# Sum of squares, layer-embedding products and row scale at the head of a one-core hybrid decoder layer

## The chip, the cores and the metric

One NeuronCore of a Trainium2 chip. The metric is device time in microseconds of one execution, the median of three runs. The engines are PE (TensorE, matmuls; its weight loads are PEld), VectorE (DVE), ScalarE (ACT), POOL (GpSimd) and SP (SyncE, which here issues the DMAs).

## The reference, cut to what matters

One layer, 512 tokens, width 1024, all in float32:

```python
hn = rms_norm(h, norm_g[i])                    # h * rsqrt(mean(h*h) + eps) * g
z = hn @ w_in[i]                               # q, k, v, gates, pooling and gating inputs
ya = moba_attention(q, k, v, rel_bias) * silu(ga)
yb = multiscale_pool(xb, pool_w[i], pool_scale[i]) * silu(gb)
yc = spatial_gating(uc, vc, sgu_w[i], sgu_b[i]) * silu(gc)
h = h + concat([ya, yb, yc]) @ w_out[i]
h = h + (p[i] @ ple_w[i]) * sigmoid(h @ ple_gate_w[i])
return rms_norm(h, final_g)
```

The change concerns three pieces at the head: the product `p[i] @ ple_w[i]` (512 x 256 by 256 x 1024, the layer embedding), the sum of squares of each row of x, and the row scale `rsqrt(mean + eps)` made from it.

## The kernel before

Every product is made of three float32r matmuls: an operand is cut into a high part (ScalarE copies it to float32r) and a low part (VectorE subtracts the high part), and high*high, high*low and low*high are summed in PSUM (`three`, lines 79 to 81). Activations lie transposed in SBUF, eight blocks `xk[k]` of 128 channels by 512 tokens.

The head runs in this order. Fourteen small matmuls warm PE up. SP loads p and the two halves of the embedding weight (`plw0`, `plw1`: output columns 0 to 511 and 512 to 1023, each with its two blocks of 128 inputs side by side) in pieces, then the eight x blocks, the value weights (`raw_0` to `raw_3`, two x blocks to a weight piece), the bias table and the q and k weights. `raw` tiles take turns in three buffers, so the first value weight waits until p's raw tile has been cut. `cut_into` makes the high and low parts of p and the weights, and `ple_mm` runs the embedding products, four banks `ps_ple0` for the first 512 columns and then `ps_ple1` for the second 512; ScalarE or VectorE copies them to `ple`.

`gain(k)` makes the high and low parts of x times the norm's gain, without the row scale. The value projection (loop over k from 0 to 7, twelve matmuls of 512 columns to a block, banks `ps_v`) runs on these unscaled parts; its rows are scaled when they are copied out (`value`). Meanwhile the row scale is made: ScalarE squares the x blocks (`sq_k`); the squares are added, partly on POOL (`sq_0` to `sq_3`), partly on VectorE; after block `SS_AT` = 3 PE multiplies the sum by a column of ones (`row_scale`, `ps_ss`); VectorE makes the mean plus epsilon (`ms`), POOL its power -0.5 (`rstd`); one block later PE widens `rstd`, one number a row, to a whole tile (`row_scale_wide`, `ps_rbc`), ScalarE copies it to `rbc`, and `rescale(k)` replaces the parts of each block by scaled ones for the q, k and other projections. Each engine runs its instructions strictly in its own order; a framework that schedules ahead of time places them, so that order is not quite the order of the code.

Of the kernel before, what the change touches and what calls it, by code (L numbers as in the profile page):

```python
# [14 lines left out]
AF = mybir.ActivationFunctionType  # L15
ALU = mybir.AluOpType

P = 128
S = 512
D = 1024  # L20
NT = S // P
KD = D // P
# [11 lines left out]
LAG = 4  # L34
HELD = 5
RATE = 1.4
SS_AT = 3


def bucket_ranges():  # L40
# [12 lines left out]
def trunk(ctx: ExitStack, tc: tile.TileContext, t: dict, out: bass.AP):  # L53
    nc = tc.nc
# [7 lines left out]
    pm = pool("pm", bufs=PM, space=bass.MemoryType.PSUM)  # L62
    pa = pool("pa", bufs=8 - PM, space=bass.MemoryType.PSUM)

    def f(ap):
        return ap.bitcast(F32)

    def bank(p, name):
        return p.tile([P, 512], F32, tag="mm" if p is pm else "at", name=name)

    def temp(name, dt=F32):
        return gen.tile([P, 512], dt, tag="t", name=name)

# [28 lines left out]
    def fetch(upto):  # L102
        while len(raws) < min(upto, len(stream)):
            raw = wp.tile([P, 1024], F32, tag="raw", name=f"raw_{len(raws)}")
            nc.sync.dma_start(raw, stream[len(raws)])
            raws.append(raw)

    last_parts, lows = [], []

    def flush():  # L110
        for z in lows:
            z()
        lows.clear()

    def low(hi, lo, raw):
        return lambda: nc.vector.tensor_tensor(lo, raw, f(hi), op=ALU.subtract)  # L116
# [15 lines left out]
    def take(n=1, ahead=3):  # L132
        j = used[0]
        used[0] += n
        flush()
        cut(max(j + n, j + ahead))
        if n > 1:
            flush()
        fetch(len(parts) + 3 - len(lows))
        return parts[j] if n == 1 else parts[j:j + n]  # L140
# [2 lines left out]
    zero = const.tile([P, 256], BF16, name="zero")  # L143
    nc.vector.memset(zero, 0.0)
    pl_raw = [wp.tile([P, 1024], F32, tag="raw", name=f"raw_{n}") for n in ("pT", "plw0", "plw1")]
    first = [slice(0, 256), slice(256, 512), slice(512, 1024)]
    for ks in first:
        nc.sync.dma_start(pl_raw[0][:, ks], t["pT"][:, ks])
        nc.sync.dma_start(pl_raw[1][:, ks], t["plw"][0][:, ks])
    nc.sync.dma_start(pl_raw[2], t["plw"][1])  # L150
    cols = const.tile([P, 10], F32, name="cols")
    nc.sync.dma_start(cols, t["cols"])
    relT = const.tile([HEADS, 32], F32, name="relT")
# [2 lines left out]
    xk = [xt[k // 2][:, (k % 2) * 512:(k % 2 + 1) * 512] for k in range(KD)]  # L156
    for k in range(4):
        nc.sync.dma_start(xk[k], t["xT"][k])
    ident = const.tile([P, P], F32, name="ident")
# [20 lines left out]
    for b, (lo_d, hi_d) in enumerate(bucket_ranges()):  # L180
        n = hi_d - lo_d + 1
        a = 511 - hi_d
# [8 lines left out]
    def gain(k):  # L191
        nc.scalar.activation(hth[:, k, :], xk[k], AF.Copy, scale=cols[:, k:k + 1])
        nc.vector.scalar_tensor_tensor(htl[:, k, :], xk[k], cols[:, k:k + 1], f(hth[:, k, :]), op0=ALU.mult, op1=ALU.subtract)

    pth, ptl = (wp.tile([P, 1024], F32R, tag=n, name=f"{n}_pT") for n in ("hi", "lo"))
    wh0, wl0 = (wp.tile([P, 1024], F32R, tag=n, name=f"{n}_plw0") for n in ("hi", "lo"))
    wh1, wl1 = (wp.tile([P, 1024], F32R, tag=n, name=f"{n}_plw1") for n in ("hi", "lo"))
    ple = [big.tile([P, D], F32, tag="ple", name=f"ple_{i}", bufs=4) for i in range(NT)]

    def ple_mm(ps, i, k, wh, wl, a=0, b=512):  # L200
        c = slice(k * 512 + i * P, k * 512 + (i + 1) * P)
        ks = slice(k * 512 + a, k * 512 + b)
        run(three(ps[:, a:b], pth[:, c], ptl[:, c], wh[:, ks], wl[:, ks], k == 0 and a == 0, k == 1 and b == 512))

    ps0 = [bank(pa, f"ps_ple0{i}") for i in range(NT)]
    for ks in first:
        cut_into(pth[:, ks], ptl[:, ks], pl_raw[0][:, ks])
        cut_into(wh0[:, ks], wl0[:, ks], pl_raw[1][:, ks])
    for i, a in ((0, 0), (1, 0), (2, 0), (3, 0), (0, 256), (1, 256), (2, 256), (3, 256)):
        ple_mm(ps0[i], i, 0, wh0, wl0, a, a + 256)  # L210
    for i, a in ((0, 0), (0, 256), (1, 0), (1, 256), (2, 0), (2, 256), (3, 0), (3, 256)):
        ple_mm(ps0[i], i, 1, wh0, wl0, a, a + 256)
    fetch(1)
    for k in (4, 5):
        nc.sync.dma_start(xk[k], t["xT"][k])
    fetch(2)
    for k in (6, 7):
        nc.sync.dma_start(xk[k], t["xT"][k])
    cut_into(wh1, wl1, pl_raw[2])
    fetch(3)  # L220
    nc.sync.dma_start(tab_d, tab)
    gain(0)
# [10 lines left out]
    for h in range(HEADS):  # L233
        b_t = big.tile([P, 512], F32, tag="B", name=f"bias_{h}", bufs=8)
        nc.sync.dma_start(b_t, bass.AP(tensor=tab_d.tensor, offset=tab_d.offset + h * TW, ap=[[1, P], [1, 512]]))
        bias.append(b_t)
    for i in range(NT):
        ps = bank(pm, f"ps_ple1{i}")
        for k in range(2):
            ple_mm(ps, i, k, wh1, wl1)  # L240
        gain(4 + i)
        nc.vector.tensor_copy(ple[i][:, 512:], ps)

    rstd = const.tile([P, NT], F32, name="rstd")
    rbc = temp("rbc")
    sq_t = [temp(f"sq_{k}") for k in range(KD)]

    def square(k):  # L250
        nc.scalar.activation(sq_t[k], xk[k], AF.Square)

    def add_up(eng, a, b):
        eng.tensor_tensor(a, a, b, op=ALU.add)

    def row_scale():
        ps = bank(pm, "ps_ss")
        for i in range(NT):
            nc.tensor.matmul(ps[:, i:i + 1], sq_t[7][:, i * P:(i + 1) * P], ones, start=True, stop=True)
        ms = const.tile([P, NT], F32, name="ms")  # L260
        nc.vector.tensor_scalar(ms, ps[:, :NT], 1.0 / D, EPS, op0=ALU.mult, op1=ALU.add)
        nc.gpsimd.tensor_tensor(rstd, ms, half, op=ALU.pow)

    def row_scale_wide():
        ps = bank(pm, "ps_rbc")
        for i in range(NT):
            nc.tensor.matmul(ps[:, i * P:(i + 1) * P], rstd[:, i:i + 1].to_broadcast([P, P]), ident, start=True, stop=True)
        nc.scalar.activation(rbc, ps, AF.Copy)

    def rescale(k):  # L270
        hn = temp(f"hn_{k}")
        nc.vector.scalar_tensor_tensor(hn, xk[k], cols[:, k:k + 1], rbc, op0=ALU.mult, op1=ALU.mult)
        nc.scalar.activation(hth[:, k, :], hn, AF.Copy)
        return low(hth[:, k, :], htl[:, k, :], hn)
# [13 lines left out]
    for k in range(KD):  # L288
        if k % 2 == 0:
            wh, wl = take(ahead=2)  # L290
            flush()
        if k == 0:
            for z in range(4):
                square(z)
            add_up(nc.gpsimd, sq_t[0], sq_t[1])
            add_up(nc.gpsimd, sq_t[0], sq_t[2])
        elif k == 1:
            square(4)
            square(5)
            add_up(nc.gpsimd, sq_t[0], sq_t[3])  # L300
            add_up(nc.vector, sq_t[5], sq_t[4])
        elif k == 2:
            square(6)
            square(7)
            add_up(nc.vector, sq_t[6], sq_t[5])
            add_up(nc.vector, sq_t[7], sq_t[6])
            add_up(nc.vector, sq_t[7], sq_t[0])
        elif k >= 5:
            for z in ((0, 1, 2), (3,), (4, 5))[k - 5]:
                lows.append(rescale(z))  # L310
                if len(lows) > 1:
                    lows.pop(0)()
        kk = k % 2
        for i in range(NT):
            run(three(vps[i], hth[:, k, i * P:(i + 1) * P], htl[:, k, i * P:(i + 1) * P],
                      wh[:, kk * 512:(kk + 1) * 512], wl[:, kk * 512:(kk + 1) * 512], k == 0, k == KD - 1))
        if k == SS_AT:
            row_scale()
        if k == SS_AT + 1:
            row_scale_wide()  # L320
    for k in (6, 7):
        lows.append(rescale(k))
        lows.pop(0)()
    flush()


# [394 lines left out]
    ps = [bank(pm, f"ps_h{m}") for m in range(2)]  # L721
# [9 lines left out]
    for m in range(2, KD):  # L731
        w = take()
        ps = bank(pm, f"ps_h{m}")
# [32 lines left out]
    ps = [bank(pa, f"ps_g0{i}") for i in range(NT)]  # L766
    for c in range(4):
        wh, wl = take()
        for k in (2 * c, 2 * c + 1):
            z = slice((k % 2) * 512, (k % 2 + 1) * 512)  # L770
# [42 lines left out]
    for i in range(NT - 1):  # L813
        ps = ticking(second(i, 0, 512, 0))
        side.append(finish(i, ps))
    i = NT - 1
    nc.gpsimd.tensor_tensor(h2[i, 0], h2[i, 0], fg[:, :512], op=ALU.mult)
    a, b = h2[i, 1][:, :256], h2[i, 1][:, 256:]
    ps = ticking(second(i, 0, 256, 0))
# [92 lines left out]
```

## Time and profile before

| What | us |
|---|---|
| median of three runs | 301.58 (301.19 to 302.85) |
| profiled execution, its own time | 301.06 |
| span of the profiled execution | 299.3 |
| PE busy | 287.9 (96%) |
| VectorE busy | 206.5 (69%) |
| ScalarE busy | 176.6 (59%) |
| POOL busy | 37.2 (12%) |

The span runs from the first to the last instruction; the profiled execution's time is 1.8 us more. A busy PE is not a PE at its peak: matmuls overlap, so what one costs is read from start to start. The granted clock of TensorE stands in the profile as a share of full speed: 1.00 is 2.4 GHz, 0.50 is 1.2 GHz. Its mean over the span is 0.987.

### The profile page before, as it was taken

To read this page: it belongs to the slowest core of one execution; us is meant where nothing else is said; L and a number is where in the kernel's file an instruction comes from. 1 tells how busy PE (TensorE), PEld (TensorE's weight loads), DVE (VectorE), ACT (ScalarE), POOL (GpSimd) and SP (SyncE) were. 2 spreads that over 40 slices of the span, in tenths; PEclk is the share of its full clock that TensorE was granted. 3 is DMA by queue.
4 is the path that set the end of the run, shared out by engine and by line. 5 is a ranking of instruction groups with operands and counts; after the bars stand their busy time and mean duration, and the time that the engine had idled before them with its cause. 6 is when DMAs were issued, how large, how long until landed. Compare 5 with 4: busy or idle time off the path is not lost.

```text
span 299.3 us, 4228 instructions
## 1 busy us (share of the span) xinstructions
PE 287.9 (96%) x1452; PEld 242.0 (81%) x1452; DVE 206.5 (69%) x496; ACT 176.6 (59%) x361; POOL 37.2 (12%) x84
## 2 busy tenths in 40 slices
PE   7898899999999999999999999999999999999990
PEld 6786788778889978888888888888888888888890
DVE  3799299876997799978967977654645352345464
ACT  4895078546778556856599999752432242385221
POOL 2695230000000210000000000000000000041021
PEclk9999799999999999999999999999999999999996
DMA  6959902332212042111231132157242313410033
GB/s 187 376 177 300 341 19 88 129 106 101 72 72 72 0 136 78 71 54 59 63 108 55 28 130 71 44 199 249 70 142 73 137 70 85 142 56 2 0 141 140
DMA packets 12789, 33.26 MB, mean 111 GB/s; under 512 B 1880, under 2 KB 2648, under 8 KB 12768
## 3 DMA queue, kind: packets, MB, share of 16 engines
q1 hardware_dynamic: 12624, 32.73, 32.3%
q8 instruction: 11, 0.18, 0.2%
q10 hardware_dynamic: 144, 0.26, 0.2%
q14 instruction: 10, 0.08, 0.1%
HBM read 30.87 MB, written 2.12 MB: 110 GB/s over the span
## 4 chain that ended last, share of the span: by engine, by line
PE 70%; DVE 12%; ACT 8%; issue 4%; DMA 2%; POOL 1%; SPq 1%; POOLq 0%; DVEq 0%; ACTq 0%
PE ps_g L81 9%; PE ps_g L80 9%; PE ps_g L79 9%; PE ps_h L80 5%; PE ps_h L79 5%; PE ps_h L81 5%; ACT kh L404 2%; PE ps_t L473 2%; DMA raw_plw<-in_plw 2%; PE ps_k L80 2%; PE ps_k L79 2%; PE ps_k L81 2%; PE ps_v L79 1%; PE ps_v L80 1%; PE ps_v L81 1%
## 5 line engine op out<-in xcount | busy, mean ns | idle before, releaser
L128 ACT ACTIVATE hi<-raw 128x1024 fp32r<-128x1024 f32 x40 | 42.1, 1056 | 44.3 <-issue 26.5
L116 DVE TENSOR_TENSOR lo<-raw,hi 128x1024 fp32r<-128x1024 f32 x40 | 50.0, 1249 | 9.1 <-ACT hi L128 8.7
L81 PE MATMUL ps_g<-hn_hi,lo 128*128 128x512 f32 x64 | 25.6, 399 | 0.0
L80 PE MATMUL ps_g<-hn_lo,hi 128*128 128x512 f32 x64 | 25.3, 396 | 0.0
L79 PE MATMUL ps_g<-hn_hi,hi 128*128 128x512 f32 x64 | 25.3, 395 | 0.0
L79 PE MATMUL ps_g<-hi,h_hi 128*128 128x512 f32 (+1 forms) x52 | 19.8, 381 | 0.0
L717 DVE TENSOR_TENSOR h<-ps_h,h 128x512 f32<-128x512 f32 x8 | 5.5, 692 | 20.5 <-PE ps_h L81 20.5
L81 PE MATMUL ps_g<-hi,h_lo 128*128 128x512 f32 (+1 forms) x52 | 19.4, 374 | 0.0
L80 PE MATMUL ps_g<-lo,h_hi 128*128 128x512 f32 (+1 forms) x52 | 19.4, 373 | 0.0
L468 POOL MEMSET ph<- 128x128 f32 x8 | 1.9, 234 | 119.4 <-PE ps_o L489 73.9
L116 DVE TENSOR_TENSOR pl<-ps_t,ph 128x128 fp32r<-128x128 f32 (+3 forms) x32 | 15.5, 484 | 0.4
L476 ACT ACTIVATE ph<-ps_t 128x128 fp32r<-128x128 f32 (+3 forms) x32 | 13.6, 426 | 2.8 <-PE ps_t L473 2.4
L80 PEld LDWEIGHTS ps_g<-hn_lo,hi 128*128 128x128 f32 x64 | 12.0, 188 | 2.3
L473 PE MATMUL ps_t<-flip,s 128*128 128x128 f32 x80 | 13.9, 272 | 0.0
L81 PEld LDWEIGHTS ps_g<-hn_hi,lo 128*128 128x128 f32 x64 | 12.0, 188 | 2.2
L79 PEld LDWEIGHTS ps_g<-hn_hi,hi 128*128 128x128 f32 x64 | 12.0, 188 | 2.1
L79 PE MATMUL ps_v<-hi,hn_hi 128*128 128x512 f32 x32 | 13.3, 414 | 0.0
L80 PE MATMUL ps_v<-lo,hn_hi 128*128 128x512 f32 x32 | 13.2, 412 | 0.0
L451 ACT ACTIVATE s<-s,st 128x128 f32<-128x128 f32 (+1 forms) x16 | 7.2, 453 | 9.9 <-DVE st L439 9.9
L454 ACT ACTIVATE s<-s,st 128x128 f32<-128x128 f32 (+1 forms) x16 | 7.2, 451 | 10.0 <-DVE st L444 9.8
L81 PE MATMUL ps_v<-hi,hn_lo 128*128 128x512 f32 x32 | 13.1, 408 | 0.0
L779 POOL TENSOR_SCALAR fg<-fg 128x1024 f32<-128x1024 f32 x1 | 3.2, 3242 | 78.3 <-ACT h L746 78.3
(227 smaller groups left out, 867.3 us busy)
## 6 DMA issues: line engine op xcount, KB each, us to landing
raw<-in_wg SPq DMA_DIRECT2D x8, 512.0 KB, 3.4
raw<-in_wo SPq DMA_DIRECT2D x8, 512.0 KB, 3.3
raw<-in_wpg SPq DMA_DIRECT2D x8, 512.0 KB, 3.3
x<-in_xT SPq DMA_DIRECT2D x8, 256.0 KB, 5.4
raw<-in_wv SPq DMA_DIRECT2D x4, 512.0 KB, 5.3
raw<-in_wq SPq DMA_DIRECT2D x4, 512.0 KB, 6.5
bias<-tab_d SPq DMA_DIRECT2D x8, 256.0 KB, 7.0
raw<-in_wk SPq DMA_DIRECT2D x4, 512.0 KB, 4.4
```

Source lines behind the costliest of these rows:

```text
L79: return [lambda: nc.tensor.matmul(ps, lh, rh, start=first, stop=False), lambda: nc.tensor.matmul(ps, lh, rl, start=False, stop=False), la ...
L80: lambda: nc.tensor.matmul(ps, lh, rl, start=False, stop=False),
L81: lambda: nc.tensor.matmul(ps, ll, rh, start=False, stop=last)]
L116: return lambda: nc.vector.tensor_tensor(lo, raw, f(hi), op=ALU.subtract)
L128: nc.scalar.activation(hi, raws[j], AF.Copy)
L404: nc.scalar.activation(kh[e][r[z]], ps[r[e]], AF.Copy)
L451: nc.scalar.activation(sc[:, :n], sc[:, :n], AF.Exp, bias=st[:, 0:1], scale=-1.0, accum_out=st[:, 1:2])
L454: nc.scalar.activation(sc[:, 256:n], sc[:, 256:n], AF.Exp, bias=st[:, 0:1], scale=-1.0, accum_out=st[:, 7:8])
L473: nc.tensor.transpose(ps[:, j * P:(j + 1) * P], probs[h, i][:, j * P:(j + 1) * P], flip)
L476: nc.scalar.activation(ph[:, :n, iq], src, AF.Copy)
L717: nc.vector.tensor_tensor(ht[m], ps, ht[m], op=ALU.add)
L779: nc.gpsimd.tensor_scalar(fg, fg, math.sqrt(D), None, op0=ALU.mult)
```

## The change

Four things. The load of the second embedding weight is split, and the eight pieces come in the order of `pl_order`; the embedding products of the first input block are done for both weights before those of the second block, over eight banks at once, and the second block's products are 512 columns wide throughout. The squares are made while x lands, ahead of the value projection, and added in one running sum on VectorE, `sq_7` holding the whole. The gains of blocks 5 to 7 move into the value loop. `SS_AT` is 2, so the ones product, the widening and the rescaling come one block earlier each. The widening uses `transpose` in place of a matmul with the identity.

```diff
-SS_AT = 3
+SS_AT = 2
...
-    first = [slice(0, 256), slice(256, 512), slice(512, 1024)]
-    for ks in first:
-        nc.sync.dma_start(pl_raw[0][:, ks], t["pT"][:, ks])
-        nc.sync.dma_start(pl_raw[1][:, ks], t["plw"][0][:, ks])
-    nc.sync.dma_start(pl_raw[2], t["plw"][1])
+    pl_src = [t["pT"], t["plw"][0], t["plw"][1]]
+    pl_order = [(0, 0, 256), (1, 0, 256), (0, 256, 512), (1, 256, 512), (2, 0, 512), (0, 512, 1024), (1, 512, 1024), (2, 512, 1024)]
+    for z, a, b in pl_order:
+        nc.sync.dma_start(pl_raw[z][:, a:b], pl_src[z][:, a:b])
...
-    for i, a in ((0, 0), (0, 256), (1, 0), (1, 256), (2, 0), (2, 256), (3, 0), (3, 256)):
-        ple_mm(ps0[i], i, 1, wh0, wl0, a, a + 256)
+    ps1 = [bank(pm, f"ps_ple1{i}") for i in range(NT)]
+    for i in range(NT):
+        ple_mm(ps1[i], i, 0, wh1, wl1)
+    for i in range(NT):
+        ple_mm(ps0[i], i, 1, wh0, wl0)
+    for i in range(NT):
+        ple_mm(ps1[i], i, 1, wh1, wl1)
     fetch(1)
-    for k in (4, 5):
+    for k in range(4, KD):
         nc.sync.dma_start(xk[k], t["xT"][k])
     fetch(2)
-    for k in (6, 7):
-        nc.sync.dma_start(xk[k], t["xT"][k])
-    cut_into(wh1, wl1, pl_raw[2])
     fetch(3)
...
+    sq_t = [temp(f"sq_{k}") for k in range(KD)]
     for i in range(NT):
-        ps = bank(pm, f"ps_ple1{i}")
-        for k in range(2):
-            ple_mm(ps, i, k, wh1, wl1)
-        gain(4 + i)
-        nc.vector.tensor_copy(ple[i][:, 512:], ps)
+        for k in (2 * i, 2 * i + 1):
+            nc.scalar.activation(sq_t[k], xk[k], AF.Square)
+            if k:
+                nc.vector.tensor_tensor(sq_t[k], sq_t[k], sq_t[k - 1], op=ALU.add)
+        if i % 2:
+            nc.vector.tensor_copy(ple[i][:, 512:], ps1[i])
+        else:
+            nc.scalar.activation(ple[i][:, 512:], ps1[i], AF.Copy)
+        if i == 1:
+            gain(4)
...
-            nc.tensor.matmul(ps[:, i * P:(i + 1) * P], rstd[:, i:i + 1].to_broadcast([P, P]), ident, start=True, stop=True)
+            nc.tensor.transpose(ps[:, i * P:(i + 1) * P], rstd[:, i:i + 1].to_broadcast([P, P]), ident)
...
-        if k == 0:
-            for z in range(4):
-                square(z)
-            add_up(nc.gpsimd, sq_t[0], sq_t[1])
-            add_up(nc.gpsimd, sq_t[0], sq_t[2])
-        elif k == 1:
-            square(4)
-            square(5)
-            add_up(nc.gpsimd, sq_t[0], sq_t[3])
-            add_up(nc.vector, sq_t[5], sq_t[4])
-        elif k == 2:
-            square(6)
-            square(7)
-            add_up(nc.vector, sq_t[6], sq_t[5])
-            add_up(nc.vector, sq_t[7], sq_t[6])
-            add_up(nc.vector, sq_t[7], sq_t[0])
-        elif k >= 5:
-            for z in ((0, 1, 2), (3,), (4, 5))[k - 5]:
+        if k < 3:
+            gain(5 + k)
+        elif k >= 4:
+            for z in ((0, 1), (2, 3), (4, 5), (6,))[k - 4]:
                 lows.append(rescale(z))
...
-    for k in (6, 7):
-        lows.append(rescale(k))
-        lows.pop(0)()
+    lows.append(rescale(7))
     flush()
```

The order in which the instructions stand on ScalarE before, ahead of the second value weight's high part `hi_1` (`sq` are squares, `hn_hi` gains, `hi_0` the first value weight's high part):

```order
L128 ACTIVATE hi_0_263<-raw_0_244 128x1024
L192 ACTIVATE hn_hi_168<-x_2_96,cols_90 128x512 x2
L251 ACTIVATE sq_1_334<-x_0_94 128x512
L251 ACTIVATE sq_2_335<-x_1_95 128x512
L128 ACTIVATE hi_1_345<-raw_1_248 128x1024
```

On ScalarE now, the same stretch (`ple` are the embedding's copies out of PSUM):

```order
L128 ACTIVATE hi_0_282<-raw_0_265 128x1024
L226 ACTIVATE ple_3_180<-ps_ple03_184 128x512
L241 ACTIVATE sq_1_311<-x_0_95 128x512
L247 ACTIVATE ple_0_177<-ps_ple10_225 128x512
L241 ACTIVATE sq_2_312<-x_1_96 128x512
L241 ACTIVATE sq_3_313<-x_1_96 128x512
L191 ACTIVATE hn_hi_169<-x_2_97,cols_91 128x512
L241 ACTIVATE sq_4_314<-x_2_97 128x512
L241 ACTIVATE sq_5_315<-x_2_97 128x512
L247 ACTIVATE ple_2_179<-ps_ple12_227 128x512
L241 ACTIVATE sq_6_316<-x_3_98 128x512
L241 ACTIVATE sq_7_317<-x_3_98 128x512
```

`hi_1` is the row behind these; between the two high parts stand eleven pieces of work where four stood.

VectorE before, from the third value weight's low part to `ms`, the mean that follows the ones product:

```order
L116 TENSOR_TENSOR lo_2_384<-raw_2_254,hi_2_383 128x1024
L254 TENSOR_TENSOR sq_6_339<-sq_6_339,sq_5_338 128x512
L254 TENSOR_TENSOR sq_7_340<-sq_7_340,sq_6_339 128x512
L116 TENSOR_TENSOR lo_3_427<-raw_3_273,hi_3_426 128x1024
L254 TENSOR_TENSOR sq_7_340<-sq_7_340,sq_0_333 128x512
L261 TENSOR_SCALAR ms_423<-ps_ss_418 128x4
```

VectorE now, from the last sum to the first scaled block (`hn_lo` are the low parts of the gains):

```order
L243 TENSOR_TENSOR sq_7_317<-sq_7_317,sq_6_316 128x512
L192 SCALAR_TENSOR_TENSOR hn_lo_170<-x_2_97,cols_91,hn_hi_169 128x512
L192 SCALAR_TENSOR_TENSOR hn_lo_170<-x_3_98,cols_91,hn_hi_169 128x512
L116 TENSOR_TENSOR lo_2_378<-raw_2_273,hi_2_377 128x1024
L192 SCALAR_TENSOR_TENSOR hn_lo_170<-x_3_98,cols_91,hn_hi_169 128x512
L261 TENSOR_SCALAR ms_402<-ps_ss_397 128x4
L116 TENSOR_TENSOR lo_3_424<-raw_3_292,hi_3_423 128x1024
```

The last sum stood right ahead of `ms`; now three low gains and a weight's low part stand between them. Ahead of the last sum stand the second value weight's low part and, ahead of that, the other six sums.

## Rows read from the trace of the kernel before

**Rows 1.** The page's line of busy time by engine.

```profile
PE 287.9 (96%) x1452; PEld 242.0 (81%) x1452; DVE 206.5 (69%) x496; ACT 176.6 (59%) x361; POOL 37.2 (12%) x84
```

**Rows 2.** Timeline of PE, embedding: start, us, line, operation, tiles, count.

```profile
7.98 0.28 PE L81 MATMUL ps_ple<-hi_plw,lo_pT 128*128 128x256 f32 x1
...
12.30 0.40 PE L79 MATMUL ps_ple<-hi_plw,hi_pT 128*128 128x512 f32 x1
...
17.77 0.39 PE L79 MATMUL ps_v<-hi,hn_hi 128*128 128x512 f32 x1
```

**Rows 3.** Timeline of PE, ones product to the first q matmul.

```profile
30.79 1.05 PE L259 MATMUL ps_ss<-ones,sq 128*128 128x1 f32 x8 [1.98 <-DVE sq L254]
31.70 0.61 PE L79 MATMUL ps_v<-hi,hn_hi 128*128 128x512 f32 x1
...
35.43 0.39 PE L79 MATMUL ps_v<-hi,hn_hi 128*128 128x512 f32 x1
...
45.22 0.39 PE L79 MATMUL ps_q<-hn_hi,hi 128*128 128x512 f32 x1
```

**Rows 4.** Chain that ended last: start, us, what. Widening, and four later transposes.

```profile
36.28 0.89 PE ps_rbc L267 x8
...
269.49 0.44 PE ps_hr L745 x4
```

**Rows 5.** Busy time by stretch; behind POOL the granted clock, DMA share, GB/s.

```profile
8.00:10.00 2.00, 1.20 (x8) 0.80 (x7) 0.69 (x1) 1.31 (x2) 0.19 (x1) 1.00 0.95 360
...
32.00:34.00 2.00, 2.00 (x6) 1.51 (x6) 1.18 (x2) 0.00 (x0) 1.88 (x1) 0.50 0.99 370
```

**Rows 6.** SP's issues, and us to landing of x block 0 and raw_0.

```profile
4.95 1.84 SPq L158 DMA_DIRECT2D x<-in_xT  x4
8.09 0.33 SPq L105 DMA_DIRECT2D raw<-in_wv  x1
...
x<-in_xT SPq DMA_DIRECT2D x1, 256.0 KB, 5.1
...
raw<-in_wv SPq DMA_DIRECT2D x1, 512.0 KB, 5.3
```

**Rows 7.** Timeline of ScalarE, 12 to 19 us.

```profile
12.54 1.09 ACT L225 ACTIVATE ple<-ps_ple 128x512 f32<-128x512 f32 x2
...
16.19 1.34 ACT L192 ACTIVATE hn_hi<-x,cols 128x512 fp32r<-128x512 f32 x2
17.41 1.15 ACT L251 ACTIVATE sq<-x 128x512 f32<-128x512 f32 x2
18.46 1.06 ACT L128 ACTIVATE hi<-raw 128x1024 fp32r<-128x1024 f32 x1
```

**Rows 8.** Timeline of VectorE, 16 to 32 us.

```profile
16.42 1.22 DVE L116 TENSOR_TENSOR lo<-raw,hi 128x1024 fp32r<-128x1024 f32 x1
17.55 1.41 DVE L193 SCALAR_TENSOR_TENSOR hn_lo<-x,cols,hn_hi 128x512 fp32r<-128x512 f32 x2
18.88 1.28 DVE L242 COPY ple<-ps_ple 128x512 f32<-128x512 f32 x2
...
23.59 1.78 DVE L254 TENSOR_TENSOR sq<-sq,sq 128x512 f32<-128x512 f32 x1
...
27.52 1.48 DVE L254 TENSOR_TENSOR sq<-sq,sq 128x512 f32<-128x512 f32 x2
...
31.88 0.16 DVE L261 TENSOR_SCALAR ms<-ps_ss 128x4 f32<-128x4 f32 x1 [1.15 <-PE ps_ss L259]
```

**Rows 9.** Timeline of POOL, 10 to 34 us.

```profile
10.85 9.27 POOL L183 COPY tab<-neg 8x1 f32<-8x1 f32 x32
20.07 1.65 POOL L414 MEMSET kl<- 64x512 f32 x3
...
21.83 4.68 POOL L254 TENSOR_TENSOR sq<-sq,sq 128x512 f32<-128x512 f32 x3
...
32.12 1.97 POOL L262 TENSOR_TENSOR rstd<-ms,half 128x4 f32<-128x4 f32 x1 [5.46 <-DVE ms L261]
```

More of the change, by code (lines that the diff above doesn't have):

```diff
@@ L205, in trunk @@
     ps0 = [bank(pa, f"ps_ple0{i}") for i in range(NT)]
-    for ks in first:
-        cut_into(pth[:, ks], ptl[:, ks], pl_raw[0][:, ks])
-        cut_into(wh0[:, ks], wl0[:, ks], pl_raw[1][:, ks])
+    pl_parts = [(pth, ptl), (wh0, wl0), (wh1, wl1)]
+    for z, a, b in pl_order:
+        cut_into(pl_parts[z][0][:, a:b], pl_parts[z][1][:, a:b], pl_raw[z][:, a:b])
     for i, a in ((0, 0), (1, 0), (2, 0), (3, 0), (0, 256), (1, 256), (2, 256), (3, 256)):
         ple_mm(ps0[i], i, 0, wh0, wl0, a, a + 256)
-    for i, a in ((0, 0), (0, 256), (1, 0), (1, 256), (2, 0), (2, 256), (3, 0), (3, 256)):
-        ple_mm(ps0[i], i, 1, wh0, wl0, a, a + 256)
+    ps1 = [bank(pm, f"ps_ple1{i}") for i in range(NT)]
[5 more added lines that the diff above has]
+        ple_mm(ps1[i], i, 1, wh1, wl1)
     fetch(1)
-    for k in (4, 5):
+    for k in range(4, KD):
         nc.sync.dma_start(xk[k], t["xT"][k])
     fetch(2)
-    for k in (6, 7):
-        nc.sync.dma_start(xk[k], t["xT"][k])
-    cut_into(wh1, wl1, pl_raw[2])
     fetch(3)
@@ L236, in trunk @@
         bias.append(b_t)
+    sq_t = [temp(f"sq_{k}") for k in range(KD)]
     for i in range(NT):
-        ps = bank(pm, f"ps_ple1{i}")
-        for k in range(2):
-            ple_mm(ps, i, k, wh1, wl1)
-        gain(4 + i)
-        nc.vector.tensor_copy(ple[i][:, 512:], ps)
+        for k in (2 * i, 2 * i + 1):
[8 more added lines that the diff above has]
+            gain(4)
     rstd = const.tile([P, NT], F32, name="rstd")
     rbc = temp("rbc")
[L248 to L254, printed above, removed]
     def row_scale():
```

## The prediction

> **What bounds the kernel now.** I read the page first: PE is busy for 287.9 us of the span of 299.3 [rows 1], so without taking matmuls away only time in which PE idles or runs slowly can be won. Next PE's own timeline over the head of the kernel, where the diff lies. It shows two places. In the layer embedding the last matmul of 256 columns on the first blocks starts at 7.98, the first matmul of 512 columns at 12.30, and the first of the value projection at 17.77 [rows 2]. The 24 matmuls of 512 columns from 12.30 to 17.77 take 0.228 us each; the 24 of 256 columns ahead of them should take half of that each, 2.73 us in all, but fill the 4.2 us from 8.10 to 12.30, because they wait for transfers and cuts. The second place is the row scale: PE idles 1.98 us for the sum of squares before the product with ones at 30.79 [rows 3], and behind it the granted clock falls from 2.4 to 1.2 GHz: 0.50 in the stretch from 32 to 34 us, while in the stretch from 8 to 10 us PE was busy for only 1.20 of 2.00 us and kept 1.00 [rows 5]. The nine matmuls from 31.70 to 35.43 took 3.73 us where nine at 0.228 take 2.05.
>
> **The change part by part.** All sums are against the profiled execution (span 299.3, time 301.06); the yardstick is the start of the q projection, 45.22 [rows 3], behind which the order on PE is the same in both programs.
>
> *Embedding.* The 24 narrow matmuls on the second block of p become 12 wide ones, the same 2.73 us, and the first half of the second weight block lands earlier and gives PE 12 matmuls to do while the rest arrives. PE is ready at 8.10 and has 36 matmuls of 0.228 us: 8.10 + 8.21 = 16.3 instead of 17.77, a gain of 1.45. Nothing in the way: by bytes, each piece is there before PE asks for it.
>
> *SP.* One more issue stands ahead of the x blocks, and the first value weight must wait for the buffer of p, whose last piece is now sixth of eight. I estimate its issue at 9.3 instead of 8.09 [rows 6], since the sixth piece ends where 1 MB has come. With 5.3 us to landing [rows 6] that is at worst 14.6; but the x blocks ahead of it hold most of that time, and they carry the same bytes, so I take 13.4 as before (8.09 + 5.3). ScalarE asks at 14.4 (below): cost 0 to 0.2. The first q weight now stands behind the eight bias loads; its cover is the second half of the value projection, up to 41, and beyond that each microsecond of lateness would cost one.
>
> *ScalarE* becomes the first link. It starts when x block 0 lands, 4.95 + 5.1 = 10.05 [rows 6]. Prices [rows 7]: two gains fill 16.19 to 17.41, 0.61 each; two squares 17.41 to 18.46, 0.525 each. Neighbouring rows overlap by about 0.12 (16.19 + 1.34 against 17.41), so a weight's high part costs 1.06 - 0.11 = 0.95 and a PSUM copy (1.09 - 0.13) / 2 = 0.48. To the end of the first high part it has four gains, one square, three copies and one high part: 5.4, so 15.4. To the end of the second one it has, all told, five gains, eight squares, six copies and two high parts: 3.05 + 4.2 + 2.9 + 1.9 = 12.05, so 22.1. Before, that high part started at 18.46; now five squares and two copies more stand ahead of it, and one gain fewer.
>
> *VectorE* takes all seven sums, in one chain in which each waits for the one before, and no sum is left on POOL. A pair of dependent sums takes 1.48, 0.74 each; one beside POOL's sums took 1.78 [rows 8]. From the first low part (15.4 + 1.13 = 16.6) come six sums (4.44), a copy (0.64) and a low gain (0.70): 22.4. Then the second weight's low part, 23.5; the last sum, 24.3; two low gains (1.33), the third weight's low part (1.13) and a low gain (0.67): 27.4. Only here stands `ms`, behind four pieces of work that it doesn't need. From `ms` to the end of POOL's power took 2.2 us before (31.88 to 32.12 + 1.97) [rows 8, 9], so `rstd` is there at 29.6.
>
> *PE in the value projection.* Blocks 0 and 1: 16.3 + 24 x 0.228 = 21.8. Block 2 waits for the second high part, 22.2, does its four high products until 23.1, waits for the low part until 23.5, and ends at 25.35. The ones product (0.91 from 30.79 to 31.70) finds the sum done a microsecond ago and ends at 26.25. Block 3 ends at 29.0, and PE waits for `rstd` until 29.65. So the wait of 1.98 gives way to three of about 0.4, 0.4 and 0.65.
>
> *Widening.* Eight passes took 0.89; four transposes of the same size later in the kernel took 0.44 on the path [rows 4]. Gain 0.45. What I take is the row; the other end is no gain, if the built transposes of a broadcast operand take two passes as well: 0.45 dearer. The Trainium skill ("TensorE: Matmul & The Clock Gate", Part 4: PE-mode transpose) gives about 275 ns for one transpose in a kernel, which would make four of them 1.1 us and the widening 0.2 dearer than before; the trace has the same length for one instruction but lets them overlap, so it decides.
>
> *Sum.* `rstd` 29.6, transposes to 30.1, four blocks of 12 matmuls (10.94): q starts at 41.0, against 45.22. Gain 4.2. As a ledger: embedding 1.45, old wait 1.98, half clock 1.7 (3.73 - 2.05), widening 0.45, together 5.6, less the three new waits of 1.4. The rescaling behind it has sixteen steps of about 0.67 on VectorE and two weight low parts of 1.13, 13 us; from 30.7 it ends near 44. Its cover is PE's four blocks and the first seven eighths of q, so the last block is asked for near 45.8; without that cover, 13 us would stand in the path. Everything later keeps its order and moves as a whole. 301.06 - 4.2 = 296.9; the median of the runs is 0.5 above the profiled execution, so **297.4 us**. Handoffs that I mis-size, x landing up to a microsecond later, or no gain from transposes move this by -0.9 to +1.4.
>
> **The rivals.**
>
> *The clock falls all the same* (chance 0.17). Two waits within 2 us of each other, 0.8 together, and 0.65 more 6 us later. For it: before, one wait of 1.98 sufficed. Against it: from 8 to 10 us PE was idle for 0.8 of 2 us and the clock stayed at 1.00 [rows 5]. Price: the same nine matmuls, 1.7 us, where PE sets the end, less if `rstd` is later anyway: 298.6 to 299.1.
>
> *No new waits* (0.08). If x lands earlier or the chain has slack that I don't see, all 5.6 come: 296.0. Against it: ScalarE's and VectorE's chains reach the second weight within 0.3 us of each other and both miss PE's 21.8, so both would have to be shorter.
>
> *The chain of sums becomes the bound and the kernel slower* (0.03). Place: VectorE from 16.6 to 22.4, where the sums now stand beside POOL's table copies (10.85 to 20.1) instead of after them. Price: if a sum beside POOL's copies (to 20.1) and memsets (to 21.7) takes 1.78 as at 23.59, each of the five that then fall there costs 1.04 more. The chain slips by 5.2; the wait at the ones product then brings the half clock back (1.7), together 6.9 against the gain of 4.2: 297.4 + 6.9 = 304.3. It decides from a slip of 2.5 with the clock lost, or 4.2 without. Against it: the low parts at 16.42 and 17.55 read two operands beside the same copies and took 1.22 and 0.70 [rows 8, 9]; only POOL's own sums stretched VectorE. The Trainium skill ("GPSIMD Engine Reference", 1. Specifications, SBUF interfaces) says that POOL contends with VectorE instructions with two SBUF inputs, without a word on what POOL runs; by that rule these sums would be stretched.
>
> *Part of it is given back* (0.06): a late value weight or a clock loss together with a longer chain, 299.6 to 301.5.
>
> **How the numbers follow.** The forecast, 296.5 to 298.5, has 0.66; the clock rival 0.17, no new waits 0.08, part given back 0.06, slower 0.03. The range holds 8 in 10 if it goes from 296.0, the end without waits, to 299.2, which takes in the clock rival. A measurement of this kernel can tell about 0.5%, 1.5 us, from no change. Faster than 300.1: forecast, clock rival, no waits and a third of the part given back, 0.92; I say 0.9. Slower than 303.1: 0.03. Between: 0.07.
>
> **What the profile of the changed kernel would show.** The first `ps_v` matmul near 16.3, if the embedding is right; the second weight's high part ending near 22.1 and its low part near 23.5; PE waits of 0.3 to 0.7 at that weight (twice) and at `ps_rbc`, none at `ps_ss`; `ms` at 27.4 behind low parts and low gains rather than right behind the ones product; four transposes in 0.44; no stretch with a granted clock of 0.5 before the tail; q near 41. The prediction is wrong if the ones product waits for a sum again, if a stretch of 1.2 GHz stands between 22 and 34 us, or if q starts near 41 and the span is not some 4 us shorter, which would mean that something behind it takes the gain back.

## The result and the profile after

The changed kernel takes 297.61 us (median of four executions, 297.53 to 298.0) against 302.11 for the kernel before, measured beside it: a ratio of 0.9855, 95% interval [0.9822, 0.9888]. The forecast was 297.4 in a range of 296.0 to 299.2. The profiled execution spans 296.0 us (before 299.3). In a later comparison it took 297.68, ratio 0.9900 [0.9881, 0.9919] against 300.88. The changed kernel's median repeats to 0.1 us, that of the kernel before differs by 1.2, so the gain is 4.5 us by the first comparison and 3.2 by the second; the profiled spans say 3.3.

The page's line of busy time, which answers [rows 1]:

```profile
PE 286.5 (97%) x1436; PEld 240.1 (81%) x1436; DVE 204.3 (69%) x498; ACT 178.0 (60%) x364; POOL 34.0 (11%) x81
```

PE's timeline from the embedding to q (start, us, line, operation, tiles, count, and in brackets the idle time ahead with what ended it), to be held against [rows 2, 3]:

```profile
8.44 0.40 PE L79 MATMUL ps_ple<-hi_plw,hi_pT 128*128 128x512 f32 x1
...
16.62 0.84 PE L79 MATMUL ps_v<-hi,hn_hi 128*128 128x512 f32 x3
...
22.93 1.20 PE L79 MATMUL ps_v<-hi,hn_hi 128*128 128x512 f32 x4 [0.33 <-ACT hi L128]
...
24.65 0.51 PE L80 MATMUL ps_v<-lo,hn_hi 128*128 128x512 f32 x1 [0.53 <-DVE lo L116]
...
26.62 0.95 PE L259 MATMUL ps_ss<-ones,sq 128*128 128x1 f32 x8
...
30.48 0.65 PE L267 MATMUL ps_rbc<-ident,rstd 128*128 128x128 f32 x4
30.89 0.48 PE L79 MATMUL ps_v<-hi,hn_hi 128*128 128x512 f32 x1
...
41.87 0.39 PE L79 MATMUL ps_q<-hn_hi,hi 128*128 128x512 f32 x1
```

The wait of 1.98 at the ones product is gone. Two short waits stand at the second value weight, as forecast, and the matmuls ahead of the widening leave 0.2 us open. The value projection begins 1.15 us earlier and q 3.35 us earlier (41.87 against 45.22); the span is 3.3 us shorter, so nothing behind q gives any of it back. The busy time by stretch shows the clock that the removed wait had taken [rows 5] back at 1.00 (the number ahead of the last two):

```profile
22.00:24.00 2.00, 1.67 (x7) 0.84 (x5) 1.90 (x3) 2.00 (x4) 0.00 (x0) 1.00 0.95 278
24.00:26.00 2.00, 1.47 (x7) 1.11 (x7) 2.00 (x4) 2.00 (x4) 0.00 (x0) 1.00 0.82 146
...
32.00:34.00 2.00, 2.00 (x11) 1.65 (x10) 2.00 (x4) 1.39 (x3) 0.00 (x0) 1.00 1.02 416
```

PE idled 0.33 and 0.53 of the four microseconds from 22 on, and kept 2.4 GHz.

The chain of waits names the links that now set when the scale is there (start, us, what):

```profile
5.45 5.21 DMA x<-in_xT
10.75 0.73 ACT hn_hi L191
...
15.28 0.95 ACT hi L128
...
20.89 1.05 ACT sq L241 x2
21.97 0.70 DVE sq L243
24.51 0.60 DVE sq L243
25.11 1.41 DVE hn_lo L192 x2
26.52 1.13 DVE lo L116
28.48 1.96 POOL rstd L262
30.48 0.65 PE ps_rbc L267 x4
```

It runs from x block 0's transfer through ScalarE, the running sum and the low parts on VectorE to POOL's power: the chain that the prediction drew, 0.7 to 1.0 us later throughout.

### The profile page after: what moved, and what is told of

Its sections match the earlier page's. It is cut to its first block, busy times and chain, and to the rows that moved or that the text cites. A ratio compares the mean times of both kernels' runs of the same rounds, so it can differ in the third digit from the quotient of the medians.

```text
span 296.0 us, 4201 instructions
## 1 busy us (share of the span) xinstructions
PE 286.5 (97%) x1436; PEld 240.1 (81%) x1436; DVE 204.3 (69%) x498; ACT 178.0 (60%) x364; POOL 34.0 (11%) x81
## 4 chain that ended last, share of the span: by engine, by line
PE 69%; DVE 11%; ACT 9%; issue 4%; POOL 2%; DMA 2%; SPq 1%; POOLq 0%; DVEq 0%; ACTq 0%
PE ps_g L81 9%; PE ps_g L80 9%; PE ps_g L79 9%; PE ps_h L81 5%; PE ps_h L80 5%; PE ps_h L79 5%; ACT kh L388 2%; PE ps_t L457 2%; DMA x<-in_xT 2%; DVE lo L116 2%; ACT hi L128 1%; PE ps_o L474 1%; PE ps_o L473 1%; PE ps_s L409 1%; PE ps_u L81 1%
## 5 line engine op out<-in xcount | busy, mean ns | idle before, releaser
L116 DVE TENSOR_TENSOR lo<-raw,hi 128x1024 fp32r<-128x1024 f32 x40 | 48.9, 1222 | 10.0 <-ACT hi L128 9.6
L116 DVE TENSOR_TENSOR pl<-ps_t,ph 128x128 fp32r<-128x128 f32 (+3 forms) x32 | 15.5, 483 | 0.4
L457 PEld LDWEIGHTS ps_t<-flip,s 128*128 128x128 f32 x80 | 10.4, 140 | 3.0
L763 POOL TENSOR_SCALAR fg<-fg 128x1024 f32<-128x1024 f32 x1 | 3.8, 3810 | 77.7 <-ACT hi L128 77.7
L446 DVE TENSOR_SCALAR s<-s,st 128x128 f32<-128x128 f32 (+3 forms) x32 | 12.2, 384 | 0.7
```

Of the source, the lines that this page charges most:

```text
L446: nc.vector.tensor_scalar(sc[:, :n], sc[:, :n], st[:, 2:3], None, op0=ALU.mult)
L457: nc.tensor.transpose(ps[:, j * P:(j + 1) * P], probs[h, i][:, j * P:(j + 1) * P], flip)
```

## The experiments

Theory A: the sums' chain alone decided the end, and the embedding and the scale's earlier place are worth nothing without it. The rival is the prediction's ledger taken literally: each term (1.45, 1.98, 1.7, 0.45) is a gain of its own. Each experiment is an edit of one of the two kernels; all compute the whole result.

**The embedding alone.** The kernel before with nothing but the new order of pieces and the eight banks.

```
-    for ks in first:
-        nc.sync.dma_start(pl_raw[0][:, ks], t["pT"][:, ks])
-        nc.sync.dma_start(pl_raw[1][:, ks], t["plw"][0][:, ks])
...
+    for z, a, b in pl_order:
+        nc.sync.dma_start(pl_raw[z][:, a:b], pl_src[z][:, a:b])
...
+    ps1 = [bank(pm, f"ps_ple1{i}") for i in range(NT)]
```

> The kernel before with the new embedding alone (piece order, eight banks). Theory A (the end of the value projection is set by the chain ScalarE - VectorE - POOL that makes the row scale, PE only waits for it): the first ps_v matmul moves from 17.8 to about 16.6, but the sum of squares still ends near 30.5, so PE's wait at the ones product grows from 2.0 to about 3, the clock falls again, and q starts where it did, 45 (span 299, time within 0.5 us of before). Theory B (each piece pays by itself, the ledger): q starts 1.15 us earlier, span 298.1.

It took 301.97 (ten executions), ratio 0.9999 [0.9965, 1.0033]. The value projection starts at 16.54, 1.23 us earlier than before, and q at 45.34, where it was. One row of PE's timeline, and two stretches:

```profile
25.93 0.79 PE L80 MATMUL ps_v<-lo,hn_hi 128*128 128x512 f32 x1 [2.30 <-DVE lo L116]
```

```profile
26.00:28.00 2.00, 2.00 (x5) 1.61 (x6) 2.00 (x3) 0.00 (x0) 0.00 (x0) 0.50 1.02 367
28.00:30.00 2.00, 2.00 (x8) 1.59 (x7) 1.90 (x3) 0.00 (x0) 0.00 (x0) 0.69 1.06 374
```

VectorE's timeline at that place, with the last sum:

```profile
20.73 2.93 DVE L192 SCALAR_TENSOR_TENSOR hn_lo<-x,cols,hn_hi 128x512 fp32r<-128x512 f32 x2
23.59 2.29 DVE L116 TENSOR_TENSOR lo<-raw,hi 128x1024 fp32r<-128x1024 f32 x1
...
30.06 0.69 DVE L254 TENSOR_TENSOR sq<-sq,sq 128x512 f32<-128x512 f32 x1
```

The same instructions in the kernel before:

```profile
20.08 1.22 DVE L116 TENSOR_TENSOR lo<-raw,hi 128x1024 fp32r<-128x1024 f32 x1
21.21 2.46 DVE L193 SCALAR_TENSOR_TENSOR hn_lo<-x,cols,hn_hi 128x512 fp32r<-128x512 f32 x2
...
30.05 0.68 DVE L254 TENSOR_TENSOR sq<-sq,sq 128x512 f32<-128x512 f32 x1
```

The wait came, with the half clock behind it, but not where theory A put it. The edit also changed the order on VectorE: the second weight's low part now stands behind the last two low gains instead of ahead of them, beside POOL's sums, and takes 2.29 instead of 1.22. PE waits for it, and not for the sum. What speaks for theory A is the last sum, which ends at 30.75 in this run as before (30.73). Without the wait of 2.30 and the 1.6 us of half clock PE would have come to the ones product near 28.7 instead of 32.58 and would have had to wait there; this is worked out and not measured. The time agrees with it whether the clock is kept or not: three of the ten executions had a mean granted clock of 0.993 to 0.995 and took 299.75 to 300.41, where the two of the kernel before with 0.992 and 0.997 took 300.24 and 299.89; seven had 0.986 to 0.990 and took 301.62 to 303.26.

**The changed kernel with the old embedding** (the same edit the other way round).

> The changed kernel with the old embedding put back (the second weight in one piece, the 24 narrow matmuls, four banks at a time); squares, running sum, early scale and transposes stay. Theory A: ps_v starts at 17.8, the waits at the second value weight and at ps_rbc shrink by as much, and q starts near 41.9 to 42.2 as in the changed kernel (span 296.0 to 296.4). Theory B: the embedding's 1.15 us is lost, span 297.2.

298.05, ratio 0.9875 [0.9824, 0.9926]: the gain without the embedding is nearly the whole. In the profiled execution PE waited longer for a weight piece (1.14, against 0.46 before: its high part starts 0.36 later, at 8.39, and PE was through its first blocks 0.32 earlier), and the clock fell in the embedding:

```profile
9.08 0.39 PE L79 MATMUL ps_ple<-hi_plw,hi_pT 128*128 128x256 f32 x1 [1.14 <-ACT hi_plw L75]
9.80 0.39 PE L80 MATMUL ps_ple<-lo_plw,hi_pT 128*128 128x256 f32 x1 [0.34 <-DVE lo_plw L76]
```

```profile
10.00:12.00 2.00, 2.00 (x14) 2.00 (x14) 1.22 (x2) 2.00 (x4) 1.74 (x5) 0.69 1.07 420
12.00:14.00 2.00, 2.00 (x11) 2.00 (x11) 1.93 (x8) 1.59 (x3) 2.00 (x11) 0.50 1.01 385
```

That execution took 299.1 us with a span of 297.3, the other three 296.89 to 298.1 with spans of 295.1 to 296.3, none above what theory A said. The interval of the ratio, 1.5 us either way, is too wide to settle the 1.15 by itself. In the new order PE would have other matmuls to do when a piece is late; no run shows what that is worth.

**The scale block back behind the fourth block** (`SS_AT = 3` in the changed kernel).

> The changed kernel with SS_AT = 3: ones product, widening and rescaling one block later, all else as changed. Theory A: the sum is there at 25.2 either way; the ones product runs at about 29.4, rstd is there before block 4 ends, so the wait at ps_rbc goes and q starts at 41.5; the rescaling starts 2 us later, ends near 47 and may cost up to 1 us inside q: span 295.7 to 297. Rival (the earlier row scale is what brings the gain): a block of 2.7 us comes back, span 298.7.

296.93, ratio 0.9833 [0.9781, 0.9885]; PE does not wait at the widening (33.02), and q starts at 41.64. The earlier place brings nothing: the block of 2.7 us that the rival would give back is not there. The four executions span 294.7 to 295.5, below those of the changed kernel, but in another comparison, so that the later place is faster is not shown.

**Widening by four plain matmuls again**, in the changed kernel.

```
-            nc.tensor.transpose(ps[:, i * P:(i + 1) * P], rstd[:, i:i + 1].to_broadcast([P, P]), ident)
+            nc.tensor.matmul(ps[:, i * P:(i + 1) * P], rstd[:, i:i + 1].to_broadcast([P, P]), ident, start=True, stop=True)
```

> The changed kernel with the widening as a matmul with the identity again. If the transposes lie on the path: eight passes of 0.11 us instead of four, q starts 0.45 us later, span 296.4 to 296.5. If they are hidden by the wait for rstd: no difference, span 296.0.

One execution, 297.89. From the widening's start to q it takes 11.91 us (29.86 to 41.77) against 11.39 (30.48 to 41.87), so 0.52 on the path; but this execution's scale was there 0.6 earlier, and the total tells nothing.

**The squares alone.** The kernel before with squares on landing and the one running sum: old embedding, scale block behind the fourth block, widening by matmuls.

> The kernel before with the squares on landing and the one running sum alone: the old embedding, the scale block back behind the fourth block and the widening by 512-column... by four plain matmuls as before. Theory A (the sums' chain decided all, the embedding and the scale's place nothing): the wait of 1.98 us at the ones product and the half clock behind it are gone, and nothing stands in their place; ps_v's first matmul to q's is the matrix engine's own 23.6 to 24.1 us, q at 41.4 to 42.3 us where ps_v starts at 17.8, and up to 43.5 where a weight piece lands late as in the run with the old embedding; time 297.0 to 298.6, ratio 0.982 to 0.990. Rival (the ledger adds up: 1.45 us of the gain belongs to the embedding and 0.45 to the widening): 299.0 to 299.6, ratio 0.991 to 0.993.

297.93, ratio 0.9893 [0.9878, 0.9908], 3.3 us faster than the kernel before in the same comparison (301.26). PE's timeline:

```profile
18.02 0.39 PE L79 MATMUL ps_v<-hi,hn_hi 128*128 128x512 f32 x1
...
29.27 0.94 PE L260 MATMUL ps_ss<-ones,sq 128*128 128x1 f32 x8
...
32.95 1.05 PE L268 MATMUL ps_rbc<-ident,rstd 128*128 128x128 f32 x8
...
42.03 0.39 PE L79 MATMUL ps_q<-hn_hi,hi 128*128 128x512 f32 x1
```

VectorE's last sum:

```profile
24.47 0.68 DVE L244 TENSOR_TENSOR sq<-sq,sq 128x512 f32<-128x512 f32 x1
```

The sum is there at 25.15 instead of 30.73, four microseconds before PE asks for it. PE works through from 18.02 to 42.03 without a wait, and q starts 0.16 later than in the whole change, although the value projection starts 1.40 later: what the embedding puts PE ahead, PE then spends waiting. From the first value matmul to q it takes 24.01 us, against 27.45 before; the difference of 3.44 is the old wait and the half clock (1.98 + 1.7) but for 0.2. Theory A holds: this part alone does nearly all of it. Embedding, earlier scale and transposes together are worth some 0.3 us (297.93 against 297.61 and 297.68, from different comparisons, so the 0.3 is not clear of noise). The part is itself at least three things: the squares come earlier, POOL sums nothing any more, and the gains of blocks 5 to 7 move into the value loop. No run tells these apart.

**The second value weight cut ahead of the later squares**, an attempt at the two waits that are left.

```
         if i == 1:
+            cut(2)
+            flush()
             gain(4)
```

> The changed kernel, but weight chunk raw_1 is cut (hi_1 on ScalarE, lo_1 on VectorE) right behind the second embedding block's copy, ahead of the squares of x blocks 4 to 7 and of their sums. If the two waits at raw_1 (0.5 for lo_1 and 0.3 for hi_1) and the gaps beside them are all that is left between ps_v and the scale: they go, and q starts 0.6 to 1.1 us earlier (40.8 to 41.3 where x lands as in the changed kernel's profile, 41.9 there), time 296.4 to 297.1. Rival: the last sum comes 2 us later for it (27.2), the ones product waits 0.6 to 1.2 us, and the clock stays: no gain, 297.4 to 298.2.

297.54, ratio 0.9889 [0.9863, 0.9915]: the time is the rival's. The two waits went, and 0.18 at the ones product (the rival said 0.6 to 1.2) and 0.66 at the widening came in their place.

**The same with the scale block behind the fourth block.**

> The same, with the scale block behind the fourth block instead of the third. No wait at raw_1 and none at the scale, since the ones product comes 3 us later; q starts at 40.4 to 41.1 where x lands as in the changed kernel's profile; time 295.9 to 296.7, the fastest of all. Rival: the rescaling of the last blocks comes late for q (three blocks less time), q's last rows wait up to 1 us: 296.7 to 297.5.

296.42, ratio 0.9842 [0.9827, 0.9856], span 294.5. PE works from 16.56 to q at 40.12, 23.56 us, without a wait; then VectorE's rescaling comes late for q (`[0.41 <-DVE hn_lo L116]` at 45.67). q stands 1.75 us earlier than in the changed kernel's profile, and 1.5 of it are left in the span. Run again beside the changed kernel:

> The version with raw_1 cut ahead of the later squares and the scale block behind the fourth block, once more, beside the changed kernel on the same chip. Its q stood 1.75 us earlier and its span 1.5 us shorter; if that is its own and not a difference of the executions, it is 0.7 to 1.5 us faster than the changed kernel here; if it is chance, within 0.4 us.

297.19 (295.77 to 298.59), ratio 0.9875 [0.9844, 0.9906]; the changed kernel there:

> The changed kernel itself, for the comparisons of this job: 297.0 to 298.0 us, ratio to the kernel before 0.984 to 0.989.

297.68, with spans from 295.4 to 296.1. Of the ten executions of this version seven span 294.1 to 295.0 and three 296.0 to 296.9. The profile is of one of the three. ScalarE and PE at its start:

```profile
5.51 0.42 ACT L75 ACTIVATE hi_plw<-raw_plw 128x256 fp32r<-128x256 f32 x1 [2.04 <-DMA raw_plw<-in_plw]
```

```profile
5.98 1.22 PE L79 MATMUL ps_ple<-hi_plw,hi_pT 128*128 128x256 f32 x4 [1.70 <-ACT hi_plw L75]
...
8.71 0.42 PE L79 MATMUL ps_ple<-hi_plw,hi_pT 128*128 128x256 f32 x1
8.92 0.41 PE L80 MATMUL ps_ple<-lo_plw,hi_pT 128*128 128x256 f32 x1
...
10.58 0.28 PE L79 MATMUL ps_ple<-hi_plw,hi_pT 128*128 128x256 f32 x1
10.70 0.28 PE L80 MATMUL ps_ple<-lo_plw,hi_pT 128*128 128x256 f32 x1
```

The second of the eight pieces, the embedding weight's first 256 columns, landed two microseconds late (in the changed kernel its high part starts at 3.59). PE waited for it, and its matmuls of 256 columns then came every 0.21 us until 10.4 and every 0.12 only from there. The value projection starts 2.6 us later than in the profile above, and the span is 2.3 longer. In the changed kernel the waits at the second weight would hide part of such a late start; no profile shows one. The version is mostly about 1 us faster; that it is faster as a whole is not shown, the intervals overlap.

**The ones column late: the price of the wait alone.** The changed kernel, with the ones written by POOL behind a row of memsets.

```
-    nc.vector.memset(ones, 1.0)
...
+    for _ in range(48):
+        nc.gpsimd.memset(zero.bitcast(F32), 0.0)
+    nc.gpsimd.tensor_scalar(ones, zero.bitcast(F32)[:, :1], 1.0, None, op0=ALU.add)
```

> The changed kernel, but the column of ones that the row sum is multiplied with is written late: by GpSimd, behind a row of small memsets that end at about 28.6 us, so that the matrix engine stands still for about 2 us at the ones product (26.6 in the changed kernel) with no other engine slowed. This measures the price of the removed wait by itself. If the wait costs its own length and the clock does not answer: the wait at the scale (0.4) is shifted with it, q at 43.5 to 44.0, time +1.6 to +2.1 over the changed kernel. Theory A's ledger (the wait brought the half clock with it, 1.7 us more): a stretch of granted clock 0.5 within 3 us behind the wait, q at 45.2 to 45.7, time +3.2 to +3.8, 300.8 to 301.4.

302.94, ratio 1.0055 [1.004, 1.007], 1.5 us beyond the dearer of the two cases, because the edit did more than I meant. The memsets moved the counter that VectorE needs early behind POOL's table copies, and VectorE's row stood still for it; PE then waited for a low part:

```profile
15.78 1.52 DVE L341 TENSOR_SCALAR icnt<-cnt 64x16 f32<-64x16 f32 x4 [4.43 <-POOL cnt L327]
```

```profile
22.02 0.50 PE L80 MATMUL ps_v<-lo,hn_hi 128*128 128x512 f32 x1 [4.71 <-DVE lo L116]
...
31.77 1.05 PE L261 MATMUL ps_ss<-ones,sq 128*128 128x1 f32 x8 [0.35 <-POOL ones L254]
```

```profile
22.00:24.00 2.00, 1.98 (x5) 1.57 (x6) 2.00 (x4) 2.00 (x3) 1.56 (x8) 0.60 0.52 129
24.00:26.00 2.00, 2.00 (x6) 1.54 (x5) 1.79 (x4) 1.72 (x3) 1.57 (x8) 0.55 0.87 215
```

It still prices a wait: from the first value matmul (16.35) to q (46.86) lie 30.51 us, 6.95 more than the 23.56 of the version without waits. The waits are 5.06 of it. The rest is 1.9, and the two stretches at 0.60 and 0.55 account for 1.7 (2 x 0.40 + 2 x 0.45). So the half clock costs as much as in the prediction's ledger, behind a wait that is more than twice as long. What a wait at the ones product costs by itself this run does not tell.

**The ones late, with no other engine's row changed.** Two POOL operations behind the last sum.

```
-    nc.vector.memset(ones, 1.0)
...
+        z = zero.bitcast(F32)[:, :1]
+        nc.gpsimd.tensor_scalar(z, sq_t[7][:, :1], 0.0, None, op0=ALU.mult)
+        nc.gpsimd.tensor_scalar(ones, z, 1.0, None, op0=ALU.add)
```

> The changed kernel with the column of ones written late again, now by two small GpSimd operations that stand behind the last sum (a column of the last sum times zero, then plus one), so that no other engine's row is changed. In the run before such an operation took 1.89 us, so the ones come about 3.8 us behind the last sum, near 29.0 us, and the matrix engine, which comes to the ones product at 26.6, waits about 2.0 to 2.5 us there. If a wait of this length costs itself alone: q 1.6 to 2.3 us later than in the changed kernel, granted clock 1.00 behind it. Theory A's ledger (it brings the half clock too, 1.7 us): clock 0.50 to 0.60 in about 4 us behind the wait, q 3.3 to 4.0 us later, time +3.3 to +4.0 over the changed kernel in the same job.

299.66 over eight executions (298.15 to 300.71), ratio 0.9953 [0.9922, 0.9984], 2.0 more than the changed kernel. The operations took 0.59 and 1.70 rather than 1.89 each, so the wait became 1.03:

```profile
27.24 1.05 PE L261 MATMUL ps_ss<-ones,sq 128*128 128x1 f32 x8 [1.03 <-POOL ones L258]
```

```profile
28.00:30.00 2.00, 2.00 (x11) 1.70 (x11) 1.30 (x2) 0.00 (x0) 1.42 (x1) 1.00 1.05 396
```

In the profiled execution the clock stayed at 1.00, and q came at 42.34, 0.5 to 0.9 later than in the two profiles of the changed kernel (41.87 and 41.40). But the executions fall into two groups: four of 298.15 to 298.94 with a mean granted clock of 0.995 or 0.996, and four of 300.37 to 300.71 with 0.989 or 0.990. The groups lie 1.9 us apart, near the price of one fall, and 0.006 of 298 us is 1.8. A wait of 1.03 us, with 0.53 three microseconds ahead of it, thus brought no fall in the profiled execution; that a fall came at this wait in the other four is likely and not shown, since none of those was profiled.

**x block 0 first.** The changed kernel with the gains' columns and x block 0 issued ahead of the last three of the eight pieces, the relative-position table behind them.

> The changed kernel, but the gains' columns and x block 0 are issued ahead of the last three weight pieces (three issues earlier), the relative-position table behind them. Theory A as mended by the result (x block 0's landing, 0.7 us later than forecast, carried the whole error): x block 0 lands 1.0 to 1.5 us earlier, ScalarE's chain and hi_1, lo_1 come 0.5 to 1.2 us earlier, the waits at raw_1 shrink to 0 to 0.3 us, q 0.5 to 1.0 us earlier (40.9 to 41.4), time -0.4 to -1.0 against the changed kernel in the same job. Rival: the cuts of the last pieces come behind the first gain and square (about 1.3 us of ScalarE) and land 0.5 us later, the embedding's second half waits for them 0.5 to 1.3 us, no gain: -0.2 to +0.8.

296.91, ratio 0.9874 [0.9852, 0.9896], against 297.68 for the changed kernel beside it. Four of its five executions span 294.4 to 294.9, where the changed kernel's span 295.4 to 296.1; by the times the forecast of 0.4 to 1.0 has it, though the intervals overlap. The profile is of the fifth, 295.9:

```profile
7.95 0.72 ACT L193 ACTIVATE hn_hi<-x,cols 128x512 fp32r<-128x512 f32 x1 [1.24 <-DMA x<-in_xT]
```

```profile
18.05 0.84 PE L79 MATMUL ps_v<-hi,hn_hi 128*128 128x512 f32 x3
```

x block 0 is there 2.8 us earlier, and from the first value matmul to q (41.78) PE has no wait. The matmuls of 256 columns ran at 0.21 us until 9.5 in this execution, and the projection began 1.4 late. In this execution the early landing did not reach the second weight: ScalarE took the cuts of the last pieces behind the first gain, as the rival said, and the second high part started at 22.07, against 21.81 in the changed kernel. PE has no wait because it came late itself. So the times suggest that x's early landing is worth 0.7 to 1 us; that it is, and by which wait, no profile shows.

## Why the prediction was right, point by point

- *Where the gain is.* Right: q moved by 3.35 us and the span by 3.3; 4.2 was forecast. That the median came out only 0.2 above the forecast is partly luck. q fell 0.9 short, which alone would have given 298.3; but the forecast had put the median 0.5 above the profiled execution, as in the kernel before, and it came 0.4 below, since the profiled execution was the slowest of its four.
- *Embedding.* 16.62 instead of 16.3. The step that missed is "PE is ready at 8.10": the first wide matmul stands at 8.44, because the first narrow matmuls came every 0.21 us until 6.4. As a length of time on PE the 1.45 was nearly right (1.15); as an entry of a ledger it was wrong. Alone the embedding gives nothing (ratio 0.9999), and without it the change keeps nearly everything.
- *SP and x.* Of the links ahead of the scale this is the one that was mis-sized. The value weight's issue came as forecast (9.41, forecast 9.3). I took x block 0 as landing where it did before (10.05) although I had counted one more issue ahead of it; its issue came at 5.45 instead of 4.95 and ScalarE's first gain at 10.75. I had priced the delay for the value weight and not for x. The 0.7 reappears in every link: second high part starting at 21.81, so ending at 22.8 (forecast 22.1), low part from 23.38 to 24.5 (23.5; the further 0.3 is the low gain at 19.40, below), `ms` at 28.24 (27.4), q at 41.87 (41.0). This is read from the profile's chain; the run with x block 0 first does not confirm it link by link.
- *ScalarE and VectorE.* The prices held: from the first gain to the second high part's end 12.0 us (forecast 12.05). Two sums beside POOL's copies took 0.68 each:

```profile
17.40 0.68 DVE L243 TENSOR_TENSOR sq<-sq,sq 128x512 f32<-128x512 f32 x1
...
18.60 0.68 DVE L243 TENSOR_TENSOR sq<-sq,sq 128x512 f32<-128x512 f32 x1
19.40 1.07 DVE L192 SCALAR_TENSOR_TENSOR hn_lo<-x,cols,hn_hi 128x512 fp32r<-128x512 f32 x1
20.39 3.07 DVE L243 TENSOR_TENSOR sq<-sq,sq 128x512 f32<-128x512 f32 x4
```

  So the slower rival (1.78 each) is out. Its rule, in the Trainium skill ("GPSIMD Engine Reference", 1. Specifications, SBUF interfaces), that POOL contends with VectorE instructions that read two SBUF inputs, did not show in these two sums beside POOL's copies of 8 partitions; it showed where POOL itself was summing [rows 8, 9]. In between lies the low gain at 19.40, which took 1.07 instead of 0.74 while POOL went from its copies to memsets of 64 partitions (19.87). With the old embedding a sum at the same place took 1.00 instead of 0.68; in some other runs nothing was stretched there.
- *PE's waits.* Forecast 0.4, 0.4 and 0.65; the idle times are 0.33, 0.53 and about 0.2, and none stands at the ones product. Read from start to start they cost 0.49, 0.92 and 0.22, and the first value weight's low part, which the forecast had free, 0.34 more (four matmuls from 16.62 to 17.87 take 1.25 where four at 0.228 take 0.91). That is 1.97 in place of 1.45, and with the 0.3 of the embedding it makes up the 0.9 by which q fell short.
- *Widening.* 0.41 from the first transpose to the next value matmul (forecast 0.44), and 0.52 more by matmuls. One transpose lasts 272 ns, near the 275 that the Trainium skill ("TensorE: Matmul & The Clock Gate", Part 4: PE-mode transpose) gives for 128x128 in bf16, where these are float32; but four of them overlap, and one pass of the plain matmuls reads 275 as well, so the length of one is no price on the path.
- *The clock.* The rival (the clock falls all the same, 0.17) did not come: every stretch from 4 to 40 us stands at 1.00. The half clock's price of 1.7 us was right: the falls seen in four traces cost 1.6 to 1.7, worked out as below.

## What to carry to other kernels

When a ledger of gains lies on one chain, first ask which entry holds the others back: here the sums' chain was worth almost the whole 3.3 us alone, and the embedding, which moved PE's work 1.2 us ahead, only changed where PE waits. Any issue that is put ahead of a transfer at the head of a critical chain must be priced for that transfer, not only for the one that waits visibly. And a wait of the matrix engine has two prices, its length and the clock that may fall behind it, so it is worth shortening even where it cannot be removed.

## What the runs showed of the hardware that was not expected

- **A fall of TensorE's clock cost nearly the same in the four profiles that show one.** Lost time is the sum over stretches of 2 us x (1 - granted clock): before, 30 to 36 us at 0.97, 0.50, 0.67, 1.7; embedding alone, 26 to 30 us at 0.50 and 0.69, 1.6; old embedding, 10 to 16 us at 0.69, 0.50 and 0.96, 1.7; first late-ones run, 1.7. The waits ahead of them were 1.98, 2.30 (with 0.69 some 8 us earlier), 1.14 with 0.34 close behind, and 4.71. Waits of 0.33 with 0.53, 0.72, and 0.66 with 0.18 brought no fall in the profiled executions, nor did 1.03 with 0.53 in the one that was profiled.
- **Time differs with the clock, without a change of code.** In the last comparison the kernel before took 299.7 to 300.34 in the five of 15 executions with 0.992 to 0.997, and 300.73 to 303.03 in the ten with 0.982 to 0.989. So part of the gain, in the median, is that the changed kernel no longer loses the clock: its nine executions have 0.992 to 0.997. But the mean clock is a sign and not a measure, since it also counts time in which PE is done: in the changed kernel's profile its whole loss lies in the last four microseconds (0.77 and 0.50, PE idle). In another comparison an execution of the kernel before with 0.992 took 301.21, as long as those with 0.986 to 0.988, and in the first late-ones run three with 0.981 and 0.982 took no longer (302.57 to 303.06) than the profiled one with 0.991 (303.0).
- **Half pace at a granted clock of 1.00.** At the kernel's start the matmuls of 256 columns came every 0.21 us, which is the pace at 1.2 GHz (256 / 1.2 GHz = 0.213; at a granted 0.50 the 512 columns of one matmul took 0.43), while the records show a granted 1.00. In most profiled executions this ended at 7.1 us or earlier, with x first at 9.5 and in the repeated cut-ahead run at 10.4, behind early waits of 0.44 and 1.70. With x first it accounts for the projection's delay of 1.4 us (some 15 matmuls at 0.09 more). Since another execution with an early wait of 0.43 was through at 6.5, the length of the wait alone does not decide it; what does stays open.
